# Norm vectors behind the split pieces, scaled copies on two engines, a longer one-tile-behind tail

## The chip, the cores and the metric

The kernel runs on one core of a Trainium2 chip. The metric is the device time of one execution in microseconds; a kernel's time is the median of its runs. A second execution was taken with the hardware profiler on; its trace is what the rows below come from.

## The reference

A small stack of layers over 256 tokens of width 1024, all in fp32. First come two blocks modulated by a conditioning vector `c`, then a third block without it. Cut to what the change touches:

```
for l in range(2):
    sh_m, sc_m, g_m, sh_f, sc_f, g_f = split(silu(c) @ ada_w[l] + ada_b[l], 6)
    h = rmsnorm(x, norm_g[l, 0]) * (1 + sc_m) + sh_m
    y = short_conv_mixer(h)  if l == 0  else  mla_mixer(h, shared_kv(x))
    x = x + g_m * rmsnorm(y, norm_g[l, 1])
    h = rmsnorm(x, norm_g[l, 2]) * (1 + sc_f) + sh_f
    y = square(relu(h @ mlp_up_w[l])) @ mlp_down_w[l]
    x = x + g_f * rmsnorm(y, norm_g[l, 3])
# second_block: x += [hgrn2(h), moba(h)] @ w_out ; x += cross_attention(h, mem) @ w_xo
#               x += square(relu(h @ w_ff1)) @ w_ff2 ; x = rms_norm(x, norm_final)
# short_conv_mixer: b, c, xh = split(h @ conv_in_w, 3);  y = (b * conv(c * xh)) @ conv_out_w
```

## The kernel before, in words

**Weights.** Every weight matrix comes as pieces of 128x1024 fp32 (512 KB). SP loads a piece into one of 7 `raw` buffers (L214); ScalarE (ACT) rounds it into `whi` (L218), VectorE (DVE) takes the rest into `wlo` (L219); 9 pairs of these buffers exist. A product is three matmuls, hi·hi, hi·lo and lo·hi, so an up or a down product needs both halves of the weight and of the activation (`hh`/`hl`, `zh`/`zl`, `mh`/`ml`). A matmul over 128x512 starts 0.23 us after the one before it.

**Two kinds of product.** `up` keeps features on the partitions, for all 256 tokens. `down` keeps tokens there: two token tiles of 128, each with two accumulators of 512 columns (acc0 and acc1 for token tile 0, acc2 and acc3 for token tile 1). There are seven downs: conv_out, attn_o, w_out_2 and w_xo_2 with 8 k-steps (one piece each), and the three MLPs' with 32. The first n - TAIL k-steps do both token tiles. In the last TAIL = 6 steps (`tail`) all of token tile 0 is finished first and token tile 1 follows, one tile behind; all pieces of the tail stay in their buffers until token tile 1 has used them.

**The norm behind a down** (`finish`, with `chain(tt)` for each token tile): sums of squares on ACT (L383), the gate on DVE (`yg`, L403), `rstd` on ACT (L393, L394), the new `x` on DVE (L407), sums and `rstd` again, `xs` on DVE (L446), four transposes by PE per half (L449), four scaled copies `h32` per half on ACT (L463, or DVE L461 for the second of two sets), `hh` on ACT (L465), `hl` on DVE (L466). Chain 0 runs while PE works on token tile 1. Three pieces of the next up (EARLY = 3) are split between the two chains, the others behind them; their products (`u`) start with token tile 0.

**Background.** The modulation vectors are `ada` steps: a 512 KB load and one DVE instruction of 1.2 us each (L342). `plan(parts, pieces)` spreads them over the coming pieces, and `mod`, `gain` and `gate_row` first flush what is still missing of their vector. `gate_row` then has PE transposes (L307) and ACT copies (L308) that make a row of it. While a tail runs, no background step is issued.

**Order.** A tile scheduler fixes each engine's order when the kernel is built, from the order of the code and from priorities (the chains are of high priority). Each engine then runs its list strictly in that order. Stages: memory keys and values, conv mixer (24 pieces of conv_in_w, conv_out), MLP 0, MLA (kv_a, q_a, kv_b, q_b, four pairs of heads, attn_o), MLP 1, the second block.

Names in the rows: `cg` the gated convolution, `zh`/`zl` its split (input of conv_out), `hkvh`/`hqh` the two normed inputs of MLA, `oh`/`ol` the attention output.

Of the kernel before, what the change touches and what calls it, by code (L numbers as in the profile page):

```python
# [27 lines left out]


MEM_PIECES = 11  # L30
BESIDE_CONV, CONV_PIECES = [(0, 2), (0, 4), (0, 3)], 28
BESIDE_MLP, MLP_PIECES = [(0, 5), ("kv", 1), ("kv", 0), (1, 1), (1, 0), (1, 2)], 54
BESIDE_MLA, MLA_PIECES = [(1, 4), (1, 3)], 20
BESIDE_MLP1, MLP1_PIECES = [(1, 5)], 30

TAIL = 6

WARM = 12

# [49 lines left out]
def net(ctx, tc, t, out):  # L89
# [94 lines left out]
    def norm_g(l, i):  # L184
        return vcol("norm_g", (l * 4 + i) * 8, 8)
# [47 lines left out]
    def piece(view, *shp):  # L233
        return split(load(view), *shp)
# [46 lines left out]
    def tail(parts, accs, last, by_half=False):  # L281

        for hf in range(2):
            for w, x, k in parts:
                down_step(w, x, accs, (0,), k == 0, k == last, (hf,))
        for hfs in ((0,), (1,)) if by_half else ((0, 1),):
            for w, x, k in parts:
                down_step(w, x, accs, (1,), k == 0, k == last, hfs)
# [67 lines left out]
    def mod(l, part):  # L356
        flush((l, part))
        base = 96 + part * 8 if l == "kv" else l * 48 + part * 8
        return mods[:, base:base + 8]

    def gate_row(l, part, i):
        g = col("gg", 8)
        nc.vector.tensor_mul(g, mod(l, part), norm_g(l, i))
        return row(g)

    def gain(l, part, g):
        a = col("gn", 8)
        nc.vector.scalar_tensor_tensor(a, mod(l, part), 1.0, g, op0=OP.add, op1=OP.mult)
        return a
# [71 lines left out]
    def modulated(tt, sets, one=False):  # L441

        r = x_rstd(tt)
        for hf in range(2):
            v = tmp("xs", 512)
            nc.vector.tensor_scalar(v, xt[tt][:, hf, :], r, None, op0=OP.mult)  # L446
            m = mtile()
            for j in range(4):
                nc.tensor.transpose(m[:, j * P:(j + 1) * P], v[:, j * P:(j + 1) * P], ident)  # L449
            sl = slice(0, P) if one else tok(tt)  # L450
            if len(sets) > 1:
                v = tmp("xf", 512)
                nc.scalar.activation(v, m, AF.Copy)
                m = v
            for i, (a, sh, h) in enumerate(sets):
                g = tmp("h32", 4, P)
                for j in range(4):
                    k = 4 * hf + j
                    x = m[:, j * P:(j + 1) * P]
                    if i:  # L460
                        nc.vector.tensor_scalar(g[:, j, :], x, a[:, k:k + 1], sh[:, k:k + 1], op0=OP.mult, op1=OP.add)  # L461
                    else:
                        nc.scalar.activation(g[:, j, :], x, AF.Identity, scale=a[:, k:k + 1], bias=sh[:, k:k + 1])  # L463
                hi = h.ks(0, 4 * hf, 4, sl)
                marks["act"] = nc.scalar.activation(hi, g, AF.Copy).ins  # L465
                marks["dve"] = nc.vector.tensor_sub(h.ks(1, 4 * hf, 4, sl), g, f32(hi)).ins  # L466


    def down(pieces, x, n, finish):

        accs = acc_pairs()
        n0 = n - TAIL
        for k in range(n0):
            down_step(piece(pieces[k], D), x(k), accs, (0, 1), k == 0, False)
        pace["hold"] = True
        ws = [piece(pieces[k], D) for k in range(n0, n)]
        tail([(ws[k - n0], x(k), k) for k in range(n0, n)], accs, n - 1)
        finish(accs)
        pace["hold"] = False
# [65 lines left out]
    def into_mlp(m, update, norm):  # L545

        h = H("h")

        def finish(accs):
            def chain(tt):  # L550
                with tc.high_priority():
                    update(tt, accs[tt])
                    norm(tt, h)

            chain(0)
            ws = [tok_pieces([m.wu[4 * b + i] for i in range(4)], EARLY if b == 0 else 0) for b in range(2)]
            chain(1)
            norm_done()
            for tt in range(2):
                for b in range(2):  # L560
                    m.first(h, tt, b, ws[b])
        return h, finish


    def softmax(sps, spans, scale, on_act=False):
# [107 lines left out]
    h = H("h")  # L673
# [33 lines left out]
    with ExitStack():  # L707
        cg = [big("cg", 4, S) for _ in range(2)]
        ub = big("upad", 2, 2, S + 2)
        upad = [ub[:, i] for i in range(2)]  # L710
        for u_ in upad:
            nc.gpsimd.memset(u_[:, :, 0:2], 0.0)
        z = H("z")

        def ev_c(hf):
            def f(pr, u):
                nc.scalar.activation(cg[hf][:, 2 * pr:2 * pr + 2, :], pair(u), AF.Copy)
            return f

        def ev_x(hf):  # L720
            def f(pr, u):
                c = cg[hf][:, 2 * pr:2 * pr + 2, :]
                nc.vector.tensor_mul(upad[pr][:, :, 2:], c, pair(u))
                for i in range(2):
                    j = 4 * hf + 2 * pr + i
                    cj = c[:, i, :]
                    nc.scalar.activation(cj, upad[pr][:, i, 0:S], AF.Identity, scale=vcol("conv_w", j),
                                         bias=vcol("conv_b", j))
                    for tap in (1, 2):
                        nc.vector.scalar_tensor_tensor(cj, upad[pr][:, i, tap:tap + S], vcol("conv_w", tap * 8 + j), cj,  # L730
                                                       op0=OP.mult, op1=OP.add)
            return f

        def ev_b(hf):
            def f(pr, u):
                c = cg[hf][:, 2 * pr:2 * pr + 2, :]
                nc.vector.tensor_mul(c, c, pair(u))
                split_into(z.ks(0, 4 * hf + 2 * pr, 2), z.ks(1, 4 * hf + 2 * pr, 2), c)
            return f

        for i, ev in enumerate([ev_c(0), ev_x(0), ev_c(1), ev_x(1), ev_b(0), ev_b(1)]):
            up([t["conv_in_w"][4 * i + j] for j in range(4)], h, ev)
        m0 = Mlp(t["mlp_up_w0"], t["mlp_down_w0"])
        g = gate_row(0, 2, 1)
        a, sh = gain(0, 4, norm_g(0, 2)), mod(0, 3)
        h, fin = into_mlp(m0, lambda tt, acc, g=g: post(tt, acc, g), lambda tt, h_, a=a, sh=sh: modulated(tt, [(a, sh, h_)]))
        down(t["conv_out_w"], lambda k: hk(z, k), 8, fin)
    plan(BESIDE_MLP, MLP_PIECES)
    lat = const.tile([P, 640], F32, name="lat")
    nc.sync.dma_start(lat, t["lat_rows"][None, :].to_broadcast([P, 640]))  # L750
# [163 lines left out]
    with tc.high_priority():  # L914
        head_pair(3)
    m1 = Mlp(t["mlp_up_w1"], t["mlp_down_w1"])
    g = gate_row(1, 2, 1)
    a, sh = gain(1, 4, norm_g(1, 2)), mod(1, 3)
    h, fin = into_mlp(m1, lambda tt, acc, g=g: post(tt, acc, g), lambda tt, h_, a=a, sh=sh: modulated(tt, [(a, sh, h_)]))
    down(t["attn_o_w"], lambda k: hk(o, k), 8, fin)  # L920
    plan(BESIDE_MLP1, MLP1_PIECES)


# [408 lines left out]
```

## Time and profile before

| | us |
|---|---|
| median of 3 runs (1038.62 to 1040.26) | 1039.99 |
| the profiled execution | 1038.09 |
| its span, first to last instruction | 1036.3 |
| PE busy | 998.1 (96%) |
| DVE busy | 736.1 (71%) |
| ACT busy | 562.0 (54%) |
| mean granted TensorE clock | 0.986 |

1.8 us of the profiled execution lie outside its span. A matmul's end is modelled, so "busy" for PE means that something was in the array; a stretch at half the clock shows as busy too. What tells where PE lost time is therefore the idle time in front of single instructions, the releaser named beside it, and the granted clock of a stretch.

### The profile page before, as it was taken

The numbers are of one execution on the slowest core, as the hardware profiler recorded it, in microseconds if no ns is written. First come the engines' busy times: TensorE is split into PE (matmuls) and PEld (weight loads), VectorE is DVE, ScalarE is ACT, GpSimd is POOL, SyncE is SP. The second block draws the span as 40 slices with busy tenths as digits, with TensorE's granted clock in tenths as the row PEclk, the third lists the DMA queues.
The fourth block names the chain that finished last, engine by engine and source line by source line (L and its number), as shares of the span: only waits on it lengthen the run. The fifth ranks groups of instructions, "written<-read, shape, count | busy, mean of one in ns | idle before, by whom it ended". The sixth has DMA issues, their size and how long they took to land.

```text
span 1036.3 us, 15870 instructions
## 1 busy us (share of the span) xinstructions
PE 998.1 (96%) x6114; PEld 873.5 (84%) x6114; DVE 736.1 (71%) x1112; ACT 562.0 (54%) x916; POOL 1.0 (0%) x8
## 2 busy tenths in 40 slices
PE   7999989999999979989999999999999999999997
PEld 6889977888998777768999888898878888988885
DVE  6888986998877689848765554868767557555542
ACT  7454448654445674768444543755455456454442
POOL 0000000000000000000000000000000000000000
PEclk8999999999999999999999999999999999999999
DMA  9889994899989269806976664673335346655611
GB/s 354 320 315 330 344 372 162 288 368 342 339 327 336 79 219 365 295 1 218 317 231 210 185 186 137 217 227 115 109 102 193 116 139 223 184 185 186 197 43 41
DMA packets 64731, 231.00 MB, mean 223 GB/s; under 512 B 7184, under 2 KB 7568, under 8 KB 64656
## 3 DMA queue, kind: packets, MB, share of 16 engines
q1 hardware_dynamic: 64512, 229.86, 64.1%
q8 instruction: 48, 0.79, 0.3%
q14 instruction: 27, 0.22, 0.1%
q10 hardware_dynamic: 144, 0.12, 0.0%
HBM read 228.91 MB, written 1.05 MB: 222 GB/s over the span
## 4 chain that ended last, share of the span: by engine, by line
PE 87%; ACT 5%; DVE 4%; DMA 2%; issue 1%; SPq 0%; ACTq 0%; DVEq 0%
PE acc L245 11%; PE acc L246 11%; PE acc L247 11%; PE u L239 11%; PE u L238 11%; PE u L240 11%; PE u L246 4%; PE u L247 4%; PE u L245 4%; PE m L250 3%; PE u L250 1%; DVE wlo L219 1%; PE acc L250 1%; DVE raw L342 1%; ACT h L463 1%
## 5 line engine op out<-in xcount | busy, mean ns | idle before, releaser
L219 DVE TENSOR_TENSOR wlo<-raw,whi 128x1024 fp32r<-128x1024 f32 (+1 forms) x317 | 380.4, 1212 | 144.0 <-ACT whi L218 140.9
L218 ACT ACTIVATE whi<-raw 128x1024 fp32r<-128x1024 f32 (+1 forms) x317 | 328.1, 1048 | 230.6 <-PE u L239 91.7
L240 PE MATMUL u<-hh,wlo 128*128 128x256 f32 x960 | 271.1, 283 | 0.0
L238 PE MATMUL u<-hh,whi 128*128 128x256 f32 x960 | 270.5, 282 | 0.0
L239 PE MATMUL u<-hl,whi 128*128 128x256 f32 x960 | 270.4, 282 | 0.0
L238 PEld LDWEIGHTS u<-hh,whi 128*128 128x128 f32 x960 | 181.3, 189 | 2.0 <-issue 1.0
L239 PEld LDWEIGHTS u<-hl,whi 128*128 128x128 f32 x960 | 180.9, 188 | 2.0 <-issue 1.0
L240 PEld LDWEIGHTS u<-hh,wlo 128*128 128x128 f32 x960 | 180.9, 188 | 1.3 <-issue 1.0
L245 PE MATMUL acc<-whi,mh 128*128 128x512 f32 x384 | 151.8, 395 | 0.0
L246 PE MATMUL acc<-whi,ml 128*128 128x512 f32 x384 | 151.5, 395 | 0.0
L247 PE MATMUL acc<-wlo,mh 128*128 128x512 f32 x384 | 151.5, 394 | 0.0
L342 DVE SCALAR_TENSOR_TENSOR raw<-raw,row 128x1024 f32<-128x1024 f32 x112 | 135.9, 1218 | 4.1 <-DMA raw<-in_adaT_dram 4.1
L247 PEld LDWEIGHTS acc<-wlo,mh 128*128 128x128 f32 x384 | 72.2, 188 | 16.9
L246 PEld LDWEIGHTS acc<-whi,ml 128*128 128x128 f32 x384 | 72.2, 188 | 15.9
L245 PEld LDWEIGHTS acc<-whi,mh 128*128 128x128 f32 x384 | 72.1, 188 | 15.9
L245 PE MATMUL u<-whi,hh 128*128 128x512 f32 x144 | 59.3, 412 | 4.9 <-ACT hh L465 4.9
L246 PE MATMUL u<-whi,hl 128*128 128x512 f32 x144 | 59.2, 411 | 0.5 <-DVE hl L466 0.4
L247 PE MATMUL u<-wlo,hh 128*128 128x512 f32 x144 | 58.4, 406 | 0.0
L245 PEld LDWEIGHTS u<-whi,hh 128*128 128x128 f32 x144 | 27.9, 194 | 11.7 <-ACT hh L465 5.6
L524 ACT ACTIVATE rl<-u 128x512 f32<-128x512 f32 x36 | 21.1, 585 | 29.5 <-PE u L240 29.5
L486 DVE TENSOR_TENSOR rq<-rl 128x512 f32<-128x512 f32 x36 | 24.7, 686 | 14.1 <-ACT rl L524 14.1
L246 PEld LDWEIGHTS u<-whi,hl 128*128 128x128 f32 x144 | 28.0, 195 | 7.2 <-DVE hl L466 1.3
(319 smaller groups left out, 1246.8 us busy)
## 6 DMA issues: line engine op xcount, KB each, us to landing
raw<-in_adaT_dram SPq DMA_DIRECT2D x112, 512.0 KB, 5.4
raw<-in_mlp_up_w_dram SPq DMA_DIRECT2D x64, 512.0 KB, 5.1
raw<-in_mlp_down_w_dram SPq DMA_DIRECT2D x64, 512.0 KB, 4.7
raw<-in_w_ff_dram SPq DMA_DIRECT2D x64, 512.0 KB, 3.6
raw<-in_w_in_dram SPq DMA_DIRECT2D x28, 512.0 KB, 4.2
raw<-in_conv_in_w_dram SPq DMA_DIRECT2D x24, 512.0 KB, 5.1
raw<-in_w_xk_dram SPq DMA_DIRECT2D x8, 512.0 KB, 7.5
raw<-in_w_xv_dram SPq DMA_DIRECT2D x8, 512.0 KB, 4.8
```

Of the source, the lines that this page charges most:

```text
L218: nc.scalar.activation(hi, view, AF.Copy)
L219: nc.vector.tensor_sub(lo, view, f32(hi))
L238: nc.tensor.matmul(o, wh, xh, start=start, stop=False, skip_group_check=True)
L239: nc.tensor.matmul(o, wh, xl, start=False, stop=False, skip_group_check=True)
L240: nc.tensor.matmul(o, wl, xh, start=False, stop=stop, skip_group_check=True)
L245: nc.tensor.matmul(o, xh, wh, start=start, stop=False, skip_group_check=True)
L246: nc.tensor.matmul(o, xl, wh, start=False, stop=False, skip_group_check=True)
L247: nc.tensor.matmul(o, xh, wl, start=False, stop=stop, skip_group_check=True)
L250: nc.tensor.matmul(o, a, b, start=start, stop=stop, skip_group_check=True)
L342: nc.vector.scalar_tensor_tensor(raw, raw, 1.0, cb, op0=OP.mult, op1=OP.mult, accum_out=mods[:, n:n + 1])
L486: nc.vector.tensor_mul(q, h_, h_)
L524: nc.scalar.activation(r, pair(u), AF.Relu)
```

## The change

`TAIL` goes from 6 to 8: in the four downs of 8 steps every step is now in the tail, in the MLPs' downs the last 8. `down` takes a function `prep` and calls it after the split pieces; for conv_out and attn_o the gate row, gain and shift of the coming norm, whose calls stood before `down`, are made there, and with them the ada steps that they flush. In `modulated`, where there is one set of vectors (the norms in front of MLP 0 and MLP 1), the four scaled copies of half 1 go to DVE. `CONV_PIECES`, over which the ada steps beside the conv mixer are spread, goes from 28 to 30.

```diff
-BESIDE_CONV, CONV_PIECES = [(0, 2), (0, 4), (0, 3)], 28
+BESIDE_CONV, CONV_PIECES = [(0, 2), (0, 4), (0, 3)], 30
...
-TAIL = 6
+TAIL = 8
...
-                    if i:
+                    if i or len(sets) == 1 and hf:
                         nc.vector.tensor_scalar(g[:, j, :], x, a[:, k:k + 1], sh[:, k:k + 1], op0=OP.mult, op1=OP.add)
                     else:
                         nc.scalar.activation(g[:, j, :], x, AF.Identity, scale=a[:, k:k + 1], bias=sh[:, k:k + 1])
...
-    def down(pieces, x, n, finish):
+    def down(pieces, x, n, finish, prep=None):
...
         ws = [piece(pieces[k], D) for k in range(n0, n)]
+        if prep:
+            prep()
         tail([(ws[k - n0], x(k), k) for k in range(n0, n)], accs, n - 1)
         finish(accs)
...
+    def gated_into_mlp(m, l):
+
+        v = {}
+
+        def prep():
+            v["g"] = gate_row(l, 2, 1)
+            v["a"], v["sh"] = gain(l, 4, norm_g(l, 2)), mod(l, 3)
+
+        h, fin = into_mlp(m, lambda tt, acc: post(tt, acc, v["g"]),
+                          lambda tt, h_: modulated(tt, [(v["a"], v["sh"], h_)]))
+        return h, fin, prep
...
-        g = gate_row(0, 2, 1)
-        a, sh = gain(0, 4, norm_g(0, 2)), mod(0, 3)
-        h, fin = into_mlp(m0, lambda tt, acc, g=g: post(tt, acc, g), lambda tt, h_, a=a, sh=sh: modulated(tt, [(a, sh, h_)]))
-        down(t["conv_out_w"], lambda k: hk(z, k), 8, fin)
+        h, fin, prep = gated_into_mlp(m0, 0)
+        down(t["conv_out_w"], lambda k: hk(z, k), 8, fin, prep)
```

The calls for MLP 1 and attn_o change in the same way.

**First place: DVE where conv_in ends and conv_out begins.** `raw_...,mods` is an ada step, `cg` the last gating, `zl` the rest of conv_out's input, `wlo` the pieces of conv_out. Before:

```order
L342 SCALAR_TENSOR_TENSOR raw_1591,mods_93<-raw_1591,row_127 128x1024
L342 SCALAR_TENSOR_TENSOR raw_1594,mods_93<-raw_1594,row_127 128x1024
L342 SCALAR_TENSOR_TENSOR raw_1597,mods_93<-raw_1597,row_127 128x1024
L737 TENSOR_TENSOR cg_728<-cg_728,u_1504 128x512
L342 SCALAR_TENSOR_TENSOR raw_1600,mods_93<-raw_1600,row_127 128x1024
L219 TENSOR_TENSOR zl_735<-cg_728,zh_733 128x512
L352 TENSOR_TENSOR mods_93<-mods_93,vec_83 128x8
L219 TENSOR_TENSOR wlo_1615<-raw_1612,whi_1614 128x1024
```

The changed kernel, same place:

```order
L219 TENSOR_TENSOR wlo_1582<-raw_1579,whi_1581 128x1024
L219 TENSOR_TENSOR zl_735<-cg_728,zh_733 128x512
L219 TENSOR_TENSOR wlo_1588<-raw_1585,whi_1587 128x1024
L219 TENSOR_TENSOR wlo_1594<-raw_1591,whi_1593 128x1024
L751 TENSOR_TENSOR cg_728<-cg_728,u_1501 128x512
L219 TENSOR_TENSOR wlo_1600<-raw_1597,whi_1599 128x1024
L368 SCALAR_TENSOR_TENSOR gn_1642<-mods_93,vec_83 128x8
L219 TENSOR_TENSOR zl_735<-cg_728,zh_733 128x512
L219 TENSOR_TENSOR wlo_1606<-raw_1603,whi_1605 128x1024
```

Four ada steps left this place, and three or four splits of conv_out now stand ahead of the last gating instead of behind it. SP's list moved alike: the eight loads of conv_out now stand ahead of the last ada loads.

**Second place: DVE in chain 0 behind conv_out**, from the first `rstd` input (`sb`) to the first `xs`. Before:

```order
L392 TENSOR_SCALAR sb_1766<-ss_1756 128x1
L403 TENSOR_TENSOR yg_1761<-acc0_1608,row_1576 128x512
L219 TENSOR_TENSOR wlo_1823<-raw_1812,whi_1822 128x1024
L403 TENSOR_TENSOR yg_1763<-acc1_1609,row_1576 128x512
L407 SCALAR_TENSOR_TENSOR x_140<-yg_1761,rstd_1765,x_140 128x512
L407 SCALAR_TENSOR_TENSOR x_140<-yg_1763,rstd_1765,x_140 128x512
L219 TENSOR_TENSOR wlo_1827<-raw_1814,whi_1826 128x1024
L392 TENSOR_SCALAR sb_1778<-ss_1772 128x1
L446 TENSOR_SCALAR xs_1782<-x_140,rstd_1777 128x512
```

The changed kernel:

```order
L392 TENSOR_SCALAR sb_1766<-ss_1756 128x1
L342 SCALAR_TENSOR_TENSOR raw_1650,mods_93<-raw_1650,row_127 128x1024
L403 TENSOR_TENSOR yg_1761<-acc0_1575,row_1629 128x512
L403 TENSOR_TENSOR yg_1763<-acc1_1576,row_1629 128x512
L407 SCALAR_TENSOR_TENSOR x_140<-yg_1761,rstd_1765,x_140 128x512
L407 SCALAR_TENSOR_TENSOR x_140<-yg_1763,rstd_1765,x_140 128x512
L342 SCALAR_TENSOR_TENSOR raw_1653,mods_93<-raw_1653,row_127 128x1024
L392 TENSOR_SCALAR sb_1778<-ss_1772 128x1
L342 SCALAR_TENSOR_TENSOR raw_1656,mods_93<-raw_1656,row_127 128x1024
L219 TENSOR_TENSOR wlo_1819<-raw_1810,whi_1818 128x1024
L446 TENSOR_SCALAR xs_1782<-x_140,rstd_1777 128x512
```

Two splits stood between `sb` and `xs`; now it is three ada steps and one split. The first two of the five ada steps stand ahead of this place, behind conv_out's last split.

**Third place: ACT in chain 0 behind MLP 0's down** (`whi` of the three early pieces of kv_a, `sq` the sums, `rstd`). Before:

```order
L218 ACTIVATE whi_3701<-raw_3695 128x960
L218 ACTIVATE whi_3705<-raw_3697 128x960
L218 ACTIVATE whi_3709<-raw_3699 128x640
L383 ACTIVATE sq_3620,ss_3619<-acc0_2063 128x512
L383 ACTIVATE sq_3622,ss_3619<-acc1_2064 128x512
L393 ACTIVATE rstd_3628<-ss_3619,sb_3629 128x1
```

The changed kernel:

```order
L218 ACTIVATE whi_3695<-raw_3689 128x960
L383 ACTIVATE sq_3614,ss_3613<-acc0_2063 128x512
L383 ACTIVATE sq_3616,ss_3613<-acc1_2064 128x512
L393 ACTIVATE rstd_3622<-ss_3613,sb_3623 128x1
L394 ACTIVATE rstd_3622<-rstd_3622 128x1
L218 ACTIVATE whi_3699<-raw_3691 128x960
L383 ACTIVATE sq_3634,ss_3633<-x_140 128x512
L218 ACTIVATE whi_3703<-raw_3693 128x640
L383 ACTIVATE sq_3636,ss_3633<-x_140 128x512
```

With eight pieces held by the tail one pair of the nine is free, and two of the three early splits moved from ahead of chain 0 into it.

## Rows read from the trace of the kernel before

**Rows 1.** The page: busy time by engine, and the chain of work that ended last by engine.

```profile
PE 998.1 (96%) x6114; PEld 873.5 (84%) x6114; DVE 736.1 (71%) x1112; ACT 562.0 (54%) x916; POOL 1.0 (0%) x8
PE 87%; ACT 5%; DVE 4%; DMA 2%; issue 1%; SPq 0%; ACTq 0%; DVEq 0%
```

**Rows 2.** What PE waited for in the whole span: us in total, times, longest.

```profile
PE u L245 <- ACT hh L465: 4.9, 2, 3.2
PE acc L245 <- ACT whi L218: 3.7, 2, 3.2
...
PE u L245 <- ACT hkvh L465: 1.7, 1, 1.7
```

**Rows 3.** The timeline where conv_in ends and conv_out begins: start, us, engine, line, operation, out<-in, [idle before <- releaser]. A row with x7 is seven instructions in a row, its time that of all.

```profile
135.96 1.22 DVE L342 SCALAR_TENSOR_TENSOR raw<-raw,row 128x1024 f32<-128x1024 f32 x1
136.02 0.28 PE L240 MATMUL u<-hh,wlo 128*128 128x256 f32 x1
...
137.11 0.68 DVE L737 TENSOR_TENSOR cg<-cg,u 128x512 f32<-128x512 f32 x1
137.83 0.63 ACT L218 ACTIVATE zh<-cg 128x512 fp32r<-128x512 f32 x1 [4.25 <-DVE cg L737]
138.36 5.85 ACT L218 ACTIVATE whi<-raw 128x1024 fp32r<-128x1024 f32 x6
...
139.46 0.50 PE L245 MATMUL acc<-whi,zh 128*128 128x512 f32 x1 [3.16 <-ACT whi L218]
...
139.53 8.03 DVE L219 TENSOR_TENSOR wlo<-raw,whi 128x1024 fp32r<-128x1024 f32 x7
```

**Rows 4.** Busy time by stretch of the span: from:to, its length, busy us of PE, PEld, DVE, ACT and POOL with their counts, the granted clock, the DMA engines' share, GB/s.

```profile
140.97:144.39 3.42, 3.42 (x10) 2.65 (x9) 3.42 (x4) 3.24 (x4) 0.00 (x0) 0.50 1.01 381
...
168.28:171.69 3.41, 3.41 (x10) 2.62 (x9) 2.93 (x6) 3.41 (x8) 0.00 (x0) 0.50 0.00 0
461.83:468.65 6.82, 5.02 (x11) 3.65 (x12) 5.28 (x10) 6.82 (x19) 0.00 (x0) 0.50 0.00 1
...
352.00:360.00 8.00, 5.46 (x32) 4.46 (x30) 7.26 (x16) 8.00 (x21) 0.00 (x0) 1.00 0.01 2
...
700.00:715.00 15.00, 13.41 (x120) 11.26 (x118) 14.15 (x31) 7.74 (x16) 0.00 (x0) 1.00 0.36 123
...
306.00:340.00 34.00, 34.00 (x199) 29.68 (x198) 25.82 (x32) 18.32 (x23) 0.00 (x0) 1.00 0.88 324
...
744.00:790.00 46.00, 45.42 (x242) 36.39 (x241) 31.63 (x71) 26.98 (x61) 0.00 (x0) 1.00 0.26 81
```

**Rows 5.** The timeline behind conv_out, columns as in rows 3: chain 0 on ACT and DVE, then PE from the end of conv_out into the first `u` products.

```profile
154.36 0.60 ACT L383 ACTIVATE sq<-acc 128x512 f32<-128x512 f32 x1 [5.64 <-PE acc L247]
...
161.24 0.88 DVE L446 TENSOR_SCALAR xs<-x,rstd 128x512 f32<-128x512 f32 x2 [0.66 <-ACT rstd L394]
...
162.67 1.85 ACT L463 ACTIVATE h<-m,mods,gn 128x128 f32<-128x128 f32 x5 [1.46 <-PE m L449]
...
165.53 0.66 ACT L465 ACTIVATE hh<-h 128x512 fp32r<-128x512 f32 x1
...
168.88 0.69 DVE L466 TENSOR_TENSOR hl<-h,hh 128x512 fp32r<-128x512 f32 x1
...
163.84 0.39 PE L246 MATMUL acc<-whi,zl 128*128 128x512 f32 x1
164.07 0.39 PE L247 MATMUL acc<-wlo,zh 128*128 128x512 f32 x1
166.24 0.51 PE L245 MATMUL u<-whi,hh 128*128 128x512 f32 x1 [1.79 <-ACT hh L465]
167.13 0.50 PE L246 MATMUL u<-whi,hl 128*128 128x512 f32 x1 [0.38 <-DVE hl L466]
```

**Rows 6.** The timeline late in MLP 0: the split of one piece of the down on DVE, and the first matmul that needs it (the third of its group of three).

```profile
320.73 1.22 DVE L219 TENSOR_TENSOR wlo<-raw,whi 128x1024 fp32r<-128x1024 f32 x1
...
329.02 0.39 PE L247 MATMUL acc<-wlo,mh 128*128 128x512 f32 x1
```

**Rows 7.** The timeline behind MLP 0's down: PE's waits at the first products of MLA.

```profile
356.44 0.41 PE L245 MATMUL u<-whi,hkvh 128*128 128x320 f32 x1 [1.66 <-ACT hkvh L465]
357.17 0.42 PE L246 MATMUL u<-whi,hkvl 128*128 128x320 f32 x1 [0.32 <-DVE hkvl L466]
...
359.96 0.44 PE L247 MATMUL u<-wlo,hqh 128*128 128x384 f32 x1 [0.56 <-DVE sb L392]
```

**Rows 8.** The timeline at attn_o: PE's first product of it, and its end.

```profile
416.04 0.50 PE L245 MATMUL acc<-whi,oh 128*128 128x512 f32 x1 [0.51 <-ACT whi L218]
...
459.27 1.11 PE L449 MATMUL m<-ident,xs 128*128 128x128 f32 x8 [0.55 <-DVE xs L446]
463.54 0.79 PE L245 MATMUL u<-whi,hh 128*128 128x512 f32 x1 [3.16 <-ACT hh L465]
```

**Rows 9.** Groups by line and shape, whole span: count | busy us, mean ns of one | idle before and releaser.

```profile
L219 DVE TENSOR_TENSOR wlo<-raw,whi 128x1024 fp32r<-128x1024 f32 x304 | 368.0, 1222 | 139.2 <-ACT whi L218 136.2 <-PE m L307 1.5
L342 DVE SCALAR_TENSOR_TENSOR raw<-raw,row 128x1024 f32<-128x1024 f32 x112 | 135.9, 1218 | 4.1 <-DMA raw<-in_adaT_dram 4.1
L463 ACT ACTIVATE h<-m,mods,gn 128x128 f32<-128x128 f32 x32 | 12.6, 465 | 7.2 <-PE m L449 7.2
L461 DVE TENSOR_SCALAR h<-xf,gn,mods 128x128 f32<-128x128 f32 x16 | 4.7, 343 | 2.0 <-ACT xf L453 2.0
```

More of the change, by code (lines that the diff above doesn't have):

```diff
@@ L916, in net @@
     m1 = Mlp(t["mlp_up_w1"], t["mlp_down_w1"])
[L917 to L920, printed above, removed]
+    h, fin, prep = gated_into_mlp(m1, 1)
+    down(t["attn_o_w"], lambda k: hk(o, k), 8, fin, prep)
     plan(BESIDE_MLP1, MLP1_PIECES)
```

## The prediction

> **What bounds the kernel now.** I read the page first: PE is busy for 96% of the span and makes up 87% of the chain that ended last [rows 1]. The reader is to see that a change which takes no matmul away can gain only where PE stands still or runs at half its clock. So the second view is what PE waited for [rows 2]: two waits for `hh`, 4.9 us together and the longest 3.2, one of 3.2 for a `whi` of a down, 1.7 for `hkvh`. The change touches all of these places. The third view is the timeline around each, the fourth the granted clock by stretch. These show that an idle time is paid twice: 3.16 us before conv_out [rows 3], and then 140.97 to 144.39 at clock 0.50 [rows 4], that is 1.2 instead of 2.4 GHz, so that 3.42 us do the work of 1.71. The same follows on the waits of 1.79 and 0.38 us behind conv_out [rows 5]: 168.28 to 171.69 at 0.50 [rows 4]. It isn't a certainty: 352 to 360 holds 2.54 us of PE idle time (8.00 less 5.46) at clock 1.00 [rows 4]. Elsewhere PE is fed: 34.00 of 34 us in 306 to 340, 45.42 of 46 around w_out_2 [rows 4].
>
> **The change part by part. Conv_out's start.** Between PE's last `up` matmul at 136.02 and its first of conv_out at 139.46 DVE runs an ada step, the last gating `cg`, another ada step, `zl`; ACT must finish `zh` behind `cg` and only then rounds conv_out's first piece, 138.36 [rows 3]. In the new order four ada steps are gone from here and three splits stand ahead of the last gating; the first piece and the first half of `z` are ready before PE asks, so the 3.16 us go, and with them the 1.71 us of clock. What is late next: DVE is full in both kernels there. From the same point of its list, about 133.0, I add 1.15 us for a split or ada step (135.96 to 137.11 for an ada step, 8.03/7 for splits [rows 3]) and 0.65 for `cg` and `zl`: second half of `zl` at 139.5, the fifth piece's `wlo` at 140.7, then one per 1.15 us against 1.4 us of PE for a piece (six matmuls of 0.23 [rows 5]). PE, which starts conv_out at 136.1, meets the fifth piece at about 140.1: a new wait of 0.5 us.
>
> **Chain 0 behind conv_out.** Token tile 0 ends at 136.1 + 48 x 0.23 + 0.5 = 147.7. Now 34 matmuls of token tile 1 stand between that and the first transposes, so PE arrives there at 155.5. On DVE the five ada steps now fall in the chain. Two run before `sb` (from 144.1 to 146.4) beside PE work and cost nothing. From `sb` at 148.1: ada, two `yg`, two `x` (152.0), ada, `sb`, ada, one split, `xs` at 155.9. Before, `sb` to `xs` held two splits, and DVE idled 0.66 us ahead of `xs` [rows 5]; now it holds four such pieces. By this walk PE waits 0.4 us; the bounds are 0 (the walk ends 0.4 early) and 2.3 (two more pieces of 1.15, none of them hidden).
>
> **The first products of MLP 0.** Before, ACT does five scaled copies (1.85 us) and, in order behind them, the sums of token tile 1 before `hh` at 165.53; PE, done with conv_out at 164.07, waits 1.79 and 0.38 [rows 5]. Now ACT has four copies, 4 x 0.465 = 1.9 us [rows 9], then `hh` (0.66), and the sums come later: 2.6 us, beside 14 matmuls (3.2 us) that still follow the first transposes. Half 1's copies run on DVE at 0.34 us each by the nearest row, which reads SBUF and not the accumulator [rows 9]; 4 x 0.34 = 1.4 against 1.9 on ACT, and both lie beside those matmuls. So both waits and their 1.71 us of clock go. What is late next is the `hl` of half 1: on DVE the two `x` updates of token tile 1 stand ahead of it, as before. Before, it ended at 169.57, 5.5 us behind the start of conv_out's last product [rows 5]; `hh` and two scaled copies stood ahead of the updates' `rstd` on ACT, 0.66 + 0.93 us, of which I count 1.3 since neighbours overlap (five copies take 1.85 and not 2.3 us). That leaves 4.2 us, and PE needs it after 13 starts, 3.0 us: a wait of 1.2 us (bounds 0 and 2). Sum for conv_out: 3.16 + 1.71 + 1.79 + 0.38 + 1.71 = 8.75, less 0.5, 0.4 and 1.2, is 6.6 us.
>
> **Does MLP 0 keep it?** The smallest lead that I find late in it is 7.1 us: a `wlo` ends at 321.95 and is first needed at 329.02 [rows 6]. If the supply doesn't come a microsecond earlier, PE still just fits in.
>
> **MLP 0's down into MLA.** The tail of eight steps puts 48 instead of 36 matmuls behind token tile 0, 2.8 us more cover for chain 0. It hides part of the 1.66 + 0.32 + 0.56 us [rows 7]. Against it, only one of nine buffer pairs is free now, and two early splits on ACT wait in the middle of chain 0 until PE has used one and two pieces of the tail, 1.4 and 2.8 us in; the second holds up the second sum by about 1 us. Also, MLA's later stages wait for chain 1, which no cover shortens. I take +0.5 (bounds -1.5 and +2.5).
>
> **Attn_o.** Its splits now stand ahead of the flushed ada steps: the 0.51 us before its first product goes [rows 8], +0.5. At its end 22 matmuls follow chain 0's beginning in both orders, so the 3.16 us before `hh` [rows 8] stay but for one scaled copy fewer ahead of it, +0.4 (bounds 0 and 3.2 + 3.4, the latter half of the 6.82 us at clock 0.50 [rows 4]).
>
> **W_out_2.** The new order leaves fewer products of token tile 0 to fill PE between the last heads' steps (two and three matmuls where seven and six stood): I take -0.5, bounds 0 and -2; no row shows it, the nearest has 0.6 us idle in 46 [rows 4]. MLP 1's and MLP 2's tails, w_xo_2 and the end of the kernel: PE waits for none of them before, and w_xo_2's heads keep their places: 0.
>
> Sum: 6.6 + 0.5 + 0.5 + 0.4 - 0.5 = 7.5 us. The profiled execution's 1038.09 (1036.3 in the span, 1.8 around it) becomes 1030.6. It lies 1.9 below the median of the runs, so on that scale I say 1032.5.
>
> **A rule that speaks against it.** The stretches 352 to 360 and 700 to 715 hold transposes and gaps at clock 1.00 [rows 4]. The Trainium skill, "TensorE: Matmul & The Clock Gate", Part 4, says that a transpose doesn't count for the clock gate as a product does; by that the half clock behind conv_out, where transposes stand among the last products, could stay with no idle time at all. Those two stretches speak against it, and I count it as a rival.
>
> **Rivals.**
> 1. Chain 0 is late. The ada steps hold up `xs` by the full 2.3 us instead of 0.4, and the clock falls behind it: 1.9 + 1.7 = 3.6 less gain, 1036.1. For it: DVE is the fuller engine there and the walk's margin is small. Against it: 0.66 us of DVE idle time in the old chain.
> 2. Transposes among products lower the clock anyway at conv_out's end: 1.7 less, 1034.2.
> 3. MLP 0 takes conv_out's gain back. The ada steps that move behind the splits push the whole supply back (three of them, 3.5 us), and the lead of 7.1 us late in MLP 0 falls short by about that or more; 0.9 is left, 1039.1. For it: DVE is the supplier. Against it: PE idles nowhere in 306 to 340 and the lead is as large as the gain.
> 4. The one free buffer pair costs more than it gives. At each down with early splits (conv_out, both MLPs, attn_o, w_out_2) ACT stands in chain 0 until PE frees a pair, `xs` comes 2.3 us late, the clock falls: 4.0 us a place. From two places on the gain of 7.5 is gone; with three it is 12 us more, 1044.5. For it: the order of ACT at MLP 0's end. Against it: the wait ends 2.8 us into 11 us of cover.
> 5. Attn_o's end gains too: `hh` comes so much earlier that idle time and half clock go there by some two thirds, 4.5 us: 1028.
>
> **How the numbers follow.** Forecast 0.52 (its own range 1030 to 1035); rivals 1 to 5: 0.17, 0.05, 0.11, 0.07, 0.08. A change of under 0.2%, 2.1 us, can't be told from none here: under 1037.9 is faster, over 1042.1 slower. The forecast, rivals 1, 2 and 5 and a little of 3 are faster, 0.83; the rest of 3 is the same, 0.10; rival 4 slower, 0.07. The range from 1027.5 to 1038.5 leaves out rival 4, half of 3 and a part of 5.
>
> **What would show it.** Right: conv_out's first product follows at once on the last `up` matmul, no stretch at clock 0.50 between 136 and 170, and the first `u` product of MLP 0 near 160.5 instead of 166.24, with that distance kept at the end of MLP 0. Rival 1 shows as PE waiting for `xs` at L449, rival 2 as clock 0.50 without idle time before it, rival 3 as waits of PE for `wlo` or `whi` within MLP 0, rival 4 as ACT idle before a `whi` released by PE in chain 0. I am wrong if the first wait goes and a later one of the same size takes its place.

## The result, and the profile after

The kernel after takes 1030.91 us, the median of 4 runs (1028.12 to 1031.75), against 1039.40 for the kernel before on the same chip: a ratio of 0.9921 [0.9905, 0.9937]. Run again later it came to 1028.06 us and 0.9908 [0.9889, 0.9927]. The change makes the kernel 0.8 to 0.9% faster. The forecast was 1032.5, with 7.5 us of gain; 8.5 were measured.

The profiled execution of after is the fastest of its four: its span of 1026.3 us is 10.0 shorter than that of before, while the medians are 8.5 apart. Terms read from this pair of traces can be too large by 1.5 us together.

The page of after first, with the rows that answer to [rows 1]: PE is busy for 3.6 us less, and idle less by the rest; its share of the chain rises from 87 to 89%.

```profile
PE 994.5 (97%) x6114; PEld 871.2 (85%) x6114; DVE 741.8 (72%) x1128; ACT 556.3 (54%) x900; POOL 1.0 (0%) x8
PE 89%; ACT 5%; DVE 3%; DMA 1%; issue 1%; SPq 0%; ACTq 0%; DVEq 0%
```

Next, what PE waited for in after (us in total, times, longest):

```profile
PE u L245 <- ACT hh L465: 2.8, 1, 2.8
...
PE m L449 <- DVE xs L446: 2.4, 2, 1.8
...
PE u L246 <- DVE hl L466: 1.2, 2, 1.0
```

Against [rows 2], the 3.7 us for `whi` and the 1.7 for `hkvh` are gone. Of the two waits for `hh` one is left, 2.8 us at attn_o. Those for `xs` (2.4 instead of 1.3) and `hl` (1.2 instead of 0.4) are longer.

The timeline of after, place by place: the start of conv_out, chain 0 from `sb` to `xs` and its transposes, PE at the first `u` products of MLP 0, the last splits of MLP 0's down and the products that need them, MLA, attn_o (columns as in [rows 3]).

```profile
135.85 0.48 PE L245 MATMUL acc<-whi,zh 128*128 128x512 f32 x1
...
138.28 4.63 DVE L219 TENSOR_TENSOR wlo<-raw,whi 128x1024 fp32r<-128x1024 f32 x4
...
145.68 0.15 DVE L392 TENSOR_SCALAR sb<-ss 128x1 f32<-128x1 f32 x1 [0.47 <-ACT sq L383]
147.27 0.60 ACT L383 ACTIVATE sq<-acc 128x512 f32<-128x512 f32 x1 [1.63 <-PE acc L247]
...
153.41 0.49 DVE L446 TENSOR_SCALAR xs<-x,rstd 128x512 f32<-128x512 f32 x1
154.97 0.60 PE L449 MATMUL m<-ident,xs 128*128 128x128 f32 x4
...
159.09 0.40 PE L245 MATMUL u<-whi,hh 128*128 128x512 f32 x1
163.49 0.50 PE L246 MATMUL u<-whi,hl 128*128 128x512 f32 x1 [1.03 <-DVE hl L466]
167.55 0.40 PE L245 MATMUL u<-whi,hh 128*128 128x512 f32 x1
...
306.94 1.23 DVE L219 TENSOR_TENSOR wlo<-raw,whi 128x1024 fp32r<-128x1024 f32 x1
315.40 0.39 PE L247 MATMUL acc<-wlo,mh 128*128 128x512 f32 x1
323.24 3.43 DVE L219 TENSOR_TENSOR wlo<-raw,whi 128x1024 fp32r<-128x1024 f32 x3 [3.63 <-ACT whi L218]
326.73 0.40 PE L247 MATMUL acc<-wlo,mh 128*128 128x512 f32 x1
...
344.91 0.31 PE L245 MATMUL u<-whi,hkvh 128*128 128x320 f32 x1
346.68 0.31 PE L245 MATMUL u<-whi,hkvh 128*128 128x320 f32 x1
350.74 0.45 PE L247 MATMUL u<-wlo,hqh 128*128 128x384 f32 x1 [0.75 <-DVE wlo L219]
356.03 0.63 PE L449 MATMUL m<-ident,xs 128*128 128x128 f32 x4 [1.79 <-DVE xs L446]
...
450.79 1.11 PE L449 MATMUL m<-ident,xs 128*128 128x128 f32 x8 [0.56 <-DVE xs L446]
453.44 0.62 ACT L383 ACTIVATE sq<-acc 128x512 f32<-128x512 f32 x1
454.01 0.66 ACT L465 ACTIVATE hh<-h 128x512 fp32r<-128x512 f32 x1
454.71 0.67 PE L245 MATMUL u<-whi,hh 128*128 128x512 f32 x1 [2.82 <-ACT hh L465]
459.26 0.39 PE L247 MATMUL u<-wlo,hh 128*128 128x512 f32 x1
```

And four rows of before's timeline that the prediction didn't need: the 31st `u` product of MLP 0, the first product of MLA, the transposes for chain 1 there, and the 12th `u` product of MLP 1.

```profile
175.53 0.39 PE L245 MATMUL u<-whi,hh 128*128 128x512 f32 x1
...
352.85 0.31 PE L245 MATMUL u<-whi,hkvh 128*128 128x320 f32 x1
...
365.27 0.63 PE L449 MATMUL m<-ident,xs 128*128 128x128 f32 x4 [0.74 <-DVE xs L446]
...
468.77 0.39 PE L247 MATMUL u<-wlo,hh 128*128 128x512 f32 x1
```

The reader is to lay the same PE instruction of both traces side by side and follow the distance:

| PE instruction | before | after | earlier by |
|---|---|---|---|
| first `u` product of MLP 0 [rows 5] | 166.24 | 159.09 | 7.15 |
| its 31st | 175.53 | 167.55 | 7.98 |
| first product of MLA, behind MLP 0's down | 352.85 | 344.91 | 7.94 |
| its 13th [rows 7] | 356.44 | 346.68 | 9.76 |
| transposes for chain 1 there | 365.27 | 356.03 | 9.24 |
| transposes at attn_o's end [rows 8] | 459.27 | 450.79 | 8.48 |
| first `u` product of MLP 1 [rows 8] | 463.54 | 454.71 | 8.83 |
| its 12th | 468.77 | 459.26 | 9.51 |
| end of the span | 1036.3 | 1026.3 | 10.0 |

Eight of ten microseconds are made at conv_out. MLP 0 passes them on whole. MLA's first products gain 1.8 more (no wait for `hkvh`); chain 1 takes 0.5 of it back (in after PE waits 0.75 us for `wlo` and 1.79 for `xs`), and the heads 0.8. Attn_o's end gives 1.0, the stages behind it the last half microsecond.

The clock by stretch in after (columns as in [rows 4]):

```profile
31.00:36.00 5.00, 4.45 (x24) 4.45 (x25) 5.00 (x8) 5.00 (x7) 0.00 (x0) 0.66 0.93 323
...
136.00:147.50 11.50, 11.50 (x51) 9.33 (x51) 10.90 (x16) 6.01 (x10) 0.00 (x0) 1.00 0.95 349
147.00:160.00 13.00, 13.00 (x62) 10.59 (x61) 11.57 (x20) 9.33 (x22) 0.00 (x0) 1.00 0.95 323
160.00:175.00 15.00, 13.97 (x65) 10.78 (x64) 13.63 (x24) 11.76 (x24) 0.00 (x0) 1.00 0.65 231
...
454.00:458.40 4.40, 3.47 (x8) 2.42 (x9) 3.40 (x9) 3.11 (x12) 0.00 (x0) 0.61 0.00 0
```

Conv_out and the first products of MLP 0 run at clock 1.00 throughout, where [rows 4] had 3.4 us at 0.50 twice. At attn_o's end a stretch at a lower clock stays, but shorter: 4.40 us at 0.61 against 6.82 at 0.50.

### The profile page after: what moved, and what is told of

Its sections match the earlier page's. It is cut to its first block, busy times and chain, and to the rows that moved or that the text cites. A ratio compares the mean times of both kernels' runs of the same rounds, so it can differ in the third digit from the quotient of the medians.

```text
span 1026.3 us, 15869 instructions
## 1 busy us (share of the span) xinstructions
PE 994.5 (97%) x6114; PEld 871.2 (85%) x6114; DVE 741.8 (72%) x1128; ACT 556.3 (54%) x900; POOL 1.0 (0%) x8
## 4 chain that ended last, share of the span: by engine, by line
PE 89%; ACT 5%; DVE 3%; DMA 1%; issue 1%; SPq 0%; ACTq 0%; DVEq 0%
PE u L238 12%; PE u L239 12%; PE u L240 12%; PE acc L245 11%; PE acc L246 11%; PE acc L247 11%; PE u L246 4%; PE u L247 4%; PE u L245 4%; PE m L250 3%; PE u L250 1%; PE acc L250 1%; ACT whi L218 1%; ACT h L463 1%; PE m L599 1%
## 5 line engine op out<-in xcount | busy, mean ns | idle before, releaser
L219 DVE TENSOR_TENSOR wlo<-raw,whi 128x1024 fp32r<-128x1024 f32 (+1 forms) x317 | 381.1, 1213 | 139.5 <-ACT whi L218 136.4
L526 ACT ACTIVATE rl<-u 128x512 f32<-128x512 f32 x36 | 21.1, 587 | 32.3 <-PE u L240 32.3
```

The lines of the kernel that those rows point to most:

```text
L219: nc.vector.tensor_sub(lo, view, f32(hi))
L526: nc.scalar.activation(r, pair(u), AF.Relu)
```

## The experiments

The theory: moving the norm vectors behind the split pieces removes the wait at conv_out's start; the tail of eight steps gives chain 0, which now holds the ada steps, cover; and neither does much alone. Rivals: one part alone makes the gain, or the copies on DVE do. Ratios are to the kernel before on the same chip.

| run | what it is | median us | ratio [95%] |
|---|---|---|---|
| prep_only | new order, tails of 6, copies on ACT | 1036.42 | 0.9981 [0.9965, 0.9997] |
| tail8_only | before, with tails of 8 | 1037.91 | 0.9999 [0.9987, 1.0011] |
| act_copies | after, copies on ACT | 1028.76 | 0.9905 [0.9888, 0.9921] |
| tail8_long | after, tails of 6 in `down` | 1034.72 | 0.9962 [0.9952, 0.9972] |
| tail8_short | after, tails of 6 in the MLPs | 1028.29 | 0.9899 [0.9882, 0.9915] |
| pieces34 | after, three more ada steps behind the splits | 1028.16 | 0.9903 [0.9885, 0.9921] |
| pieces24 | after, all those ada steps in conv_in | 1032.71 | 0.9949 [0.9933, 0.9965] |
| sums_late | after, sums of chain 1 behind `hh`, `hl` | 1027.04 | 0.9892 [0.9876, 0.9907] |
| sums_late_again | the same kernel again | 1028.36 | 0.9897 [0.9881, 0.9913] |
| sums_late_act | sums_late, copies on ACT | 1029.90 | 0.9920 [0.9903, 0.9937] |
| halves | sums_late, two copies of each half on DVE | 1029.33 | 0.9908 [0.9892, 0.9924] |

**The new order alone, and the tail alone.** Of after, for the first:

```diff
-TAIL = 8
+TAIL = 6
...
-                    if i or len(sets) == 1 and hf:
+                    if i:
```

and of before, for the second:

```diff
-TAIL = 6
+TAIL = 8
```

> The kernel before with one part of the change: the norm vectors worked out behind the split pieces (and the pacing over 30 pieces). The tail stays at 6 steps and all scaled copies on ScalarE. My theory, that the parts need each other: the 3.16 us wait before conv_out and the half clock behind it go (4.9 us), but chain 0 now holds two ada steps and three splits on VectorE between sb and xs, with only 36 matmuls of token tile 1 as cover, all of them ahead of the transposes; PE then waits about 1 us for xs and some 3.4 us for hh where it waited 1.79 and 0.38. First product of MLP 0 near 164 instead of 166.24, the clock at half behind it as before: 2 to 3 us faster than before in all, about 1037. The rival, that the parts add up: conv_out's wait and clock are worth 4.9 us by themselves, 1034.5.

> The kernel before with the tail of 8 steps alone; vectors and ada steps stand before the downs as before, all scaled copies on ScalarE. My theory: the wait of 3.16 us before conv_out and its half clock stay as they are (nothing of what ACT and VectorE do ahead of the first piece has moved), the wait at the first product of MLP 0 stays at 1.5 to 2.5 us since only four matmuls follow the second transposes and the sums still stand ahead of hh; behind MLP 0's down and at attn_o up to 1 us is gained each: 0 to 2 us faster, about 1038.5. The rival, that the longer tail is the main part: the waits behind conv_out go with their clock (3.9 us) and those at MLA, 1034 to 1035.

The new order alone, timeline:

```profile
158.27 1.03 PE L449 MATMUL m<-ident,xs 128*128 128x128 f32 x8
162.48 0.51 PE L245 MATMUL u<-whi,hh 128*128 128x512 f32 x1 [3.18 <-ACT hh L465]
```

The wait at conv_out's start is gone (136 to 142 is busy for 6.00 of 6.00 us), but the wait for `hh` grows from 1.79 [rows 5] to 3.18. With the ada steps in chain 0 the order has all of conv_out's products ahead of the transposes: eight of these in a row, and then nothing for PE to do while the copies and `hh` are made. Before has six products of conv_out behind the first transposes, after fourteen. The first `u` product comes 3.76 us earlier than before, and in this trace all of that is lost again by the end.

The tail alone:

```profile
137.08 0.79 PE L245 MATMUL acc<-whi,zh 128*128 128x512 f32 x1 [3.17 <-ACT whi L218]
164.83 0.50 PE L245 MATMUL u<-whi,hh 128*128 128x512 f32 x1 [1.53 <-ACT hh L465]
```

```profile
158.00:168.00 10.00, 8.08 (x38) 5.97 (x37) 6.05 (x12) 8.16 (x24) 0.00 (x0) 1.00 0.28 97
```

The first wait stays, with a lower clock behind it (0.61 in 137 to 145). The wait for `hh` shrinks by only 0.26 us: seven products follow the first transposes instead of six, and ACT still has the sums of token tile 1 ahead of `hh`.

What each is worth where the change was aimed shows between two PE instructions that all traces have, the first product of conv_in and the 31st `u` product of MLP 0:

| trace | first product of conv_in | 31st `u` product | between |
|---|---|---|---|
| before | 66.96 | 175.53 | 108.57 |
| new order alone | 66.80 | 171.53 | 104.73 |
| tail alone | 64.58 | 172.57 | 107.99 |
| after | 66.77 | 167.55 | 100.78 |

The new order alone saves 3.8 us there, the tail alone 0.6, both together 7.8. In both runs the distance then shrinks by 3 to 3.5 us in the stage of the heads ahead of attn_o. There the tail alone has a wait of 2.0 us for `pexp`, and the clock falls in both: 0.70 in 410 to 415 with the new order, 0.57 in 412 to 420 with the tail, where before and after have 1.00. The new order's profiled execution (1038.41) is one of its slowest: its ten runs lie between 1033.28 and 1039.15. So 0.2% and nothing alone, 0.8 to 0.9% together: the parts need each other, and no part makes the gain. At conv_out the traces show why; why the heads lose in each was not traced to its end.

**Which tail.** Of after, tails of six in `down` (conv_out, attn_o, w_out_2 and w_xo_2), and, apart from it, in the MLPs' downs:

```diff
-        n0 = n - TAIL
+        n0 = n - 6
```

```diff
-            n0 = 4 * nb - TAIL
+            n0 = 4 * nb - 6
```

> The changed kernel with the longer tail only in the MLPs' downs; the downs of 8 steps keep their tail of 6, with the vectors behind the split pieces. My theory, as prep_only showed: conv_out's first wait goes, a wait of some 3.3 us for hh with half the clock comes behind it since all products stand ahead of the transposes, and at attn_o the heads lose 3 us: ratio 0.996 to 0.999. The rival, that prep_only lost its gain at MLP 0's down for want of the longer tail there: as the changed kernel but for 2 us, 0.993 to 0.994.

> The changed kernel with the longer tail only in the downs of 8 steps (conv_out, attn_o, w_out_2, w_xo_2); the MLPs' downs keep their tail of 6. My theory: all of conv_out's gain stays; behind MLP 0's down the waits of 1.66 + 0.32 us for hkvh and hkvl return, but chain 1 sets the end of that stage, so it is within 0.7 us of the changed kernel there: ratio 0.991 to 0.993. The rival, that the MLPs' tails give 2 us and more: 0.9935 and up.

Short tails in `down`, timeline:

```profile
160.87 0.49 PE L245 MATMUL u<-whi,hh 128*128 128x512 f32 x1 [2.83 <-ACT hh L465]
```

Half of the gain goes: again no product of conv_out stands behind the transposes, the wait for `hh` is back with 2.83 us, and a lower clock behind it (0.72 in 160 to 166). Between the two instructions of the table this trace has 104.84 us (65.56 to 170.40), as the new order alone. Short tails in the MLPs cost nothing that can be measured. Their timeline:

```profile
347.15 0.41 PE L245 MATMUL u<-whi,hkvh 128*128 128x320 f32 x1 [1.69 <-ACT hkvh L465]
...
356.56 0.63 PE L449 MATMUL m<-ident,xs 128*128 128x128 f32 x4 [0.76 <-DVE xs L446]
```

The wait for `hkvh` is back, and the one for `xs` is 0.76 instead of 1.79. Against before this trace is 9.3 us early at the first product of MLA (343.54), 8.7 at chain 1's transposes and 9.4 at attn_o's end (449.92); after is 7.9, 9.2 and 8.5. So the longer tail saves 1.9 us up to chain 1's transposes, and by attn_o's end 0.5 of that is left, too little for these runs to show.

**The copies.** Of after, all scaled copies of a lone norm back on ACT (the second edit of prep_only).

> The changed kernel with all scaled copies back on ScalarE. My theory: at conv_out 14 matmuls (3.2 us) still cover five copies and hh (1.85 + 0.66), so nothing is lost there; at attn_o hh comes one copy (0.3 to 0.45 us) later, and the clock with it. Within 1 us of the changed kernel, 1031 to 1032. The rival, that the second engine is what takes the waits behind conv_out away: 1.79 + 0.38 us and 1.7 us of clock return, 1034.5.

No loss. At conv_out the 1.03 us for `hl` even go, and the wait for `hh` at attn_o is longer by 0.3 (3.16). The copies on two engines are no part of the gain.

**How many ada steps lie ahead.**

```diff
-BESIDE_CONV, CONV_PIECES = [(0, 2), (0, 4), (0, 3)], 30
+BESIDE_CONV, CONV_PIECES = [(0, 2), (0, 4), (0, 3)], 34
```

and 24 in place of 34 for the other.

> The changed kernel with the ada steps beside the conv mixer spread over 34 pieces instead of 30, so that eight instead of five of them are left for behind conv_out's splits, six of them on VectorE between sb and xs (three in the changed kernel). My theory, that chain 0's margin on VectorE is about one ada step (xs was done 1.07 us before PE's transposes were due): PE waits for xs 3 x 1.15 - 1.07 = 2.4 us, and 1 us more where its late arrival meets nothing else; with the clock at half for a while behind it 2.4 to 4 us slower than the changed kernel, ratio 0.9945 to 0.996. The rival, that VectorE has slack in chain 0 beyond that, or that the conv mixer gains what chain 0 loses: no difference.

> The changed kernel with the ada steps spread over conv_in's 24 pieces, so that none is left for behind conv_out's splits. My theory: what matters is that no ada step stands ahead of the last gating and of conv_out's splits; pacing them into conv_in takes them out of chain 0 but adds five steps (5.8 us of VectorE) to a stage whose splits lead PE by only 0.3 to 2.3 us: PE waits there for wlo, 2 to 5 us in all, and the result is 1 to 4 us slower than the changed kernel, ratio 0.993 to 0.996. The rival, that late is no better than early as long as they are not flushed in one go: the same time as the changed kernel, 0.992.

With 34, eight ada steps follow the splits, six of them between `sb` and `xs`, and still PE doesn't wait:

```profile
145.19 0.60 ACT L383 ACTIVATE sq<-acc 128x512 f32<-128x512 f32 x1 [4.87 <-PE acc L247]
151.74 0.48 DVE L446 TENSOR_SCALAR xs<-x,rstd 128x512 f32<-128x512 f32 x1
153.35 0.60 PE L449 MATMUL m<-ident,xs 128*128 128x128 f32 x4
```

DVE is done with the splits earlier and runs the extra steps while PE is still at token tile 0 (`sb` comes at 140.75, the sum of acc1 at 145.19); `xs` comes even 1.7 us earlier than after's 153.41. What I had taken for a margin of one ada step isn't one. With 24, the waits on PE and the stretch of conv_in:

```profile
PE u L240 <- DVE wlo L219: 3.2, 5, 1.1
```

```profile
60.00:134.00 74.00, 70.76 (x565) 68.34 (x564) 67.15 (x104) 34.75 (x43) 0.00 (x0) 1.00 0.93 335
```

PE stands for 3.2 us of conv_in's 74, waiting for splits that share DVE with the ada steps. Of the places tried, behind conv_out's splits is the cheapest.

**The sums of chain 1.** In after, ACT runs token tile 1's two sums (`sq`, to 454.06) between the scaled copies and `hh`, which PE awaits. Sums_late puts them behind:

```diff
-                    update(tt, accs[tt])
+                    with ExitStack() as st_:
+                        if tt:
+                            st_.enter_context(tc.issue_after(marks["act"]))
+                            st_.enter_context(tc.issue_after(marks["dve"]))
+                        update(tt, accs[tt])
```

> The changed kernel with one order more: in the norms in front of MLP 0 and MLP 1 the sums, gate products and x updates of token tile 1 are issued behind hh and hl of token tile 0. My theory: the 1.03 us wait for hl in the first products of MLP 0 goes, and at attn_o hh no longer waits for the two sums (454.01 less 452.87, 1.1 us): 1.5 to 2.5 us less than the changed kernel, about 1029. The rival: chain 1 is then late by as much and PE waits there instead, no gain, 1031.

> The changed kernel with chain 1's sums, gate products and x updates behind hh and hl of token tile 0, once more, beside the others of this group. My theory: ratio to the kernel before of 0.989 to 0.990, below the changed kernel's 0.991 to 0.992. The rival, that the first 0.9892 was luck: 0.991 to 0.992.

The timeline of each at attn_o's end, sums_late first:

```profile
452.94 0.50 PE L245 MATMUL u<-whi,hh 128*128 128x512 f32 x1 [1.80 <-ACT hh L465]
```

```profile
454.09 0.80 PE L245 MATMUL u<-whi,hh 128*128 128x512 f32 x1 [1.80 <-ACT hh L465]
```

The wait is 1.80 us instead of 2.82, in both, and the 1.03 us for `hl` in MLP 0 are gone; chain 1's own `hh` there now costs 0.3. Its two ratios, 0.9892 and 0.9897, lie below after's two, 0.9921 and 0.9908; the intervals overlap. It is the fastest version here, by a margin that these runs don't settle, and the traces don't settle it either: sums_late ends 1.1 us ahead of after (1025.2 against 1026.3), but at the first product of conv_in, ahead of all that differs, it is already 1.25 ahead (65.52 against 66.77).

Two variants of the copies on top of it:

```diff
-                    if i or len(sets) == 1 and hf:
+                    if i or len(sets) == 1 and j > 1:
```

for halves, and all on ACT for sums_late_act.

> sums_late, with the four scaled copies of each half shared two and two by ScalarE and VectorE, instead of half 0 on ScalarE and half 1 on VectorE. My theory: at attn_o hh needs two copies and itself on ScalarE (0.9 + 0.65 us) behind the transposes, but the order puts two copies of half 1 ahead of it, so it comes as late as with four; PE's wait of 1.96 us there stays within 0.3 us, and the time within 0.5 us of sums_late. The rival, that VectorE's help shortens the way to hh whatever the order: 0.6 us less wait there, and 0.5 to 2 us less time with the clock.

> The changed kernel with chain 1's sums, gate products and x updates behind hh and hl of token tile 0, and all scaled copies back on ScalarE. My theory, that the order of the sums matters and the second engine hardly: at conv_out no wait behind either set of products, at attn_o hh comes one copy later than with DVE's help (0.3 us plus clock). 0.3 to 1 us slower than sums_late, 1.5 us faster than the changed kernel: ratio 0.990. The rival, that DVE's copies are what lets hh come early: attn_o's wait grows by 1 us or more and the gain over the changed kernel is gone, 0.992.

Halves, timeline:

```profile
451.57 1.50 ACT L463 ACTIVATE h<-m,mods,gn 128x128 f32<-128x128 f32 x4 [1.27 <-PE m L449]
453.23 1.33 ACT L465 ACTIVATE hh<-h 128x512 fp32r<-128x512 f32 x2 [0.16 <-DVE h L461]
453.92 0.51 PE L245 MATMUL u<-whi,hh 128*128 128x512 f32 x1 [1.92 <-ACT hh L465]
```

ACT still runs four copies in a row ahead of `hh`, two of each half, so the wait is 1.92 and not shorter. With all copies on ACT the wait grew by only 0.2 us, to 2.00; that run lost 1.1 us elsewhere, at a wait for `rq` in MLP 0 that wasn't followed up. Its ratio fits the rival's number, but not at the place where the rival put it.

**After once more.** The same kernel, to see how far the runs scatter:

> The changed kernel itself once more, beside the others of this group. Both theories: ratio to the kernel before of 0.992 (0.9905 to 0.9937 the first time).

Its six runs lie between 1026.92 and 1031.53, as widely as the gap between most versions above.

## Why the prediction was right

**Conv_out's start: right.** The first product follows on the last transposes without a gap, at 135.85, and the clock holds. The 0.5 us for the fifth piece didn't come, and 136 to 147.5 is busy for 11.50 of 11.50 us. The four `wlo` from 138.28 follow each other in 1.16 us each, as forecast; what was off is where the walk began. It put the first of these splits at 133.0, and in after that one starts at 131.65, so that the fifth piece's `wlo` was done near 139.5 and not at 140.7. PE's side of that sum doesn't add up either: 136.1 and four pieces of 1.4 us make 141.7, not 140.1.

**Chain 0: right, with rival 1 wrong.** `xs` was to end at 155.9 and ended at 153.90; PE's transposes at 154.97 wait for nothing. Between `sb` and `xs` stand three ada steps and a split, as forecast, and the stretch took 8.2 us where the walk had 7.8. The step that failed is its start. I put all of it behind the end of token tile 0, `sb` at 148.1. But `sb` needs only the sum of acc0, which the tail finishes ahead of acc1: it ran at 145.68, and an ada step was done before the sum of acc1 began at 147.27. So the 0.4 us, and the bound of 2.3, were nothing; in pieces34, with three ada steps more, `sb` comes 4.4 us ahead of that sum, and they aren't seen either.

**First products of MLP 0: right.** The two waits and their half clock are gone; the first `u` product was to come near 160.5 and came at 159.09. The new wait for `hl` of half 1 was put at 1.2 us and measures 1.03. From the first product of conv_in on, where after is 0.2 us ahead, conv_out gives 7.8 us instead of 6.6: the waits of 0.5 and 0.4 that didn't occur are most of the difference. The copies on DVE, which read the accumulator here, took 0.41 us each instead of the 0.34 of the nearest row.

**MLP 0 keeps it: the result right, the reason wrong.** I let the gain use up a lead of 7.1 us. In after the smallest lead ahead of the down's tail is still 7.2 (306.94 + 1.23 to 315.40), though PE comes 8 us earlier: the supply moved forward with it, and rival 3 had nothing to stand on. What moved it wasn't tested. It isn't a `whi` waiting for PE to free its buffer: in 190 to 345 none does. ACT waits there for PE's `up` products (`rl`, 32.3 us in 11 times), and the splits stand behind that in its list. Within the tail the lead is nearly gone, which I hadn't seen: the last two of its eight pieces are rounded behind ACT's copies of the gate row, and their `wlo` are done 1.6 and 1.1 us before PE needs them (the last at 326.73). Before, all six of the tail stood ahead of those copies. PE waits for neither.

**MLP 0's down into MLA: +0.5 forecast, +0.5 in the trace (7.94 to 8.48), not in the runs.** The wait for `hkvh` does go, and chain 1 and the heads give most of it back. Tail8_short shows that the tail there makes no difference that can be measured. Rival 4, the buffer pairs, costs nothing visible: in chain 0 of conv_out, MLP 0 and attn_o no `whi` of after waits for PE, and the kernel with two more pairs held at each MLP can't be told from the one without.

**Attn_o.** The 0.51 us before its first product [rows 8] were to go; in after its first product waits 0.5 for `oh`, so +0.5 became 0. At its end I counted 0.4, one copy, and 1.0 was measured (8.48 at the transposes to 9.51 at the 12th `u` product of MLP 1). The wait for `hh` shrank by just that copy (3.16 to 2.82); the rest is the clock behind it, which I had left as it was. From the first to the 12th `u` product before takes 5.23 us and after 4.55, where 11 starts of 0.23 us would be 2.5. The term was mis-sized, and what came lies between it and rival 5, whose 4.5 us didn't come.

**W_out_2: −0.5 forecast, nothing lost.** Over its products the distance goes from 9.9 us (751.27 against 741.38 at the first) to 10.0 (781.62 against 771.61 at the last); it doesn't shrink.

**Rival 2.** In 147 to 160 of after eight transposes stand among the last products of conv_out, at clock 1.00. By the rule that transposes don't count for the clock gate (the Trainium skill, "TensorE: Matmul & The Clock Gate", Part 4) the clock could have fallen there; this trace shows no sign of it. That is a weak test, with eight transposes among 62 instructions, and so was the one in the prediction: of its two stretches 352 to 360 holds no transpose (four end at 351.85, the next begin at 362.34), and 700 to 715 holds four.

**The sum: nearer than its terms.** In the traces, from the first product of conv_in on, 9.8 us were gained and not 7.5: 1.2 more at conv_out, 0.6 more at attn_o's end, 0.6 more at w_out_2, 0.5 less at attn_o's start, the rest in places that the prediction put at nothing. The medians, 8.5 apart, lie nearer to the forecast because the profiled execution of after is its fastest. That nearness is luck in part, and it confirms no single term.

What the prediction did not say is how far the two parts need each other; it gives no time for either alone. Without the longer tail conv_out gives 3.8 of its 7.8 us, because no product is left behind the transposes and PE waits 3.18 us for `hh`.

## What to carry to other kernels

Before moving vector work off one wait, ask which chain it lands in and whether the matmuls beside that chain are as long as the chain has become; if not, lengthen the cover in the same change, because each alone can show nothing. On an engine that takes its work in order, look for instructions of the next tile ahead of the one that TensorE awaits: here two sums ahead of `hh` are 1.0 us of waiting, though no clear gain in time. A wait removed ahead of another chain can turn up again behind it: of the 1.9 us saved ahead of chain 1 in MLA 0.5 were left at attn_o's end. And before two traces are compared by where they end, lay the same instruction of both side by side ahead of the first thing that differs.

## What the runs showed of the hardware

An idle time of PE doesn't set a price by itself. Sums_late and its repeat have the same order and the same wait of 1.80 us for `hh`; the stretches of the first, then of the second:

```profile
31.00:36.00 5.00, 4.17 (x35) 4.17 (x36) 5.00 (x9) 5.00 (x9) 0.00 (x0) 1.00 0.93 331
412.00:420.00 8.00, 6.90 (x32) 4.75 (x31) 8.00 (x22) 3.28 (x10) 0.00 (x0) 1.00 0.95 330
453.00:462.00 9.00, 8.78 (x30) 6.78 (x31) 8.16 (x13) 8.00 (x16) 0.00 (x0) 0.81 0.30 100
```

```profile
412.00:420.00 8.00, 6.90 (x25) 4.93 (x25) 8.00 (x21) 3.28 (x10) 0.00 (x0) 0.79 0.93 335
453.00:462.00 9.00, 7.91 (x21) 5.99 (x22) 7.46 (x13) 7.86 (x17) 0.00 (x0) 0.62 0.15 57
```

In 412 to 420 PE is busy for 6.90 us in both, and does 32 instructions at clock 1.00 or 25 at 0.79. The two executions end 2.1 us apart (1026.98 and 1029.09). In 31 to 36, where nothing was changed, after has 0.66 and sums_late 1.00; that, and not the edit, is where sums_late's trace gets ahead of after's. With the tail alone the wait of 1.53 us for `hh` was followed by clock 1.00, where 1.79 us were followed by 0.50 before [rows 4, 5]. So the 1.71 us that I charged for an idle time are a chance and not a price. Where the clock falls and where it doesn't was not settled here.
